# Longer DMA rows, three output places and a later logits load in a top-2 expert dispatch kernel

## The chip, the cores and the metric

The kernel runs on one core of a Trainium2 chip. The metric is device time in microseconds, the median of several runs. Before the change it is 243.29 us (three runs, 243.09 to 243.54). The core has engines that compute (here VectorE, called DVE, and a little ScalarE, called ACT), an engine that issues transfers (SyncE, called SP), and 16 DMA engines that move data between HBM and the on-chip memory (SBUF, 128 partitions). TensorE is not used.

## The reference

`x` is 16 x 1024 tokens of 512 floats, `router_logits` has 8 floats for each token, and `k` is 2. For each token the two largest of the 8 softmax values are taken, normalised to sum to one, and the token's row of `x` is written out twice, once times each of the two weights:

```python
probs = np.exp(router_logits - logits_max)
probs = probs / np.sum(probs, axis=-1, keepdims=True)
topk_indices = np.argsort(probs, axis=-1)[..., -k:]
topk_probs = np.take_along_axis(probs, topk_indices, axis=-1)
topk_probs = topk_probs / np.sum(topk_probs, axis=-1, keepdims=True)
x_expanded = x[:, :, np.newaxis, :].repeat(k, axis=2)
return (x_expanded * topk_probs[..., np.newaxis]).astype(np.float32)
```

So 33.55 MB of `x` and 0.52 MB of logits are read and 67.11 MB are written. With two values left, the normalised weights are the sigmoid of plus and minus their difference, and that is how the kernel gets them.

## The kernel before

The 16,384 tokens are laid over the 128 partitions, 128 consecutive tokens to each, so a partition reads one contiguous stretch of 256 KB of `x` and writes one contiguous stretch of 512 KB of the output. A "row" below is one token's 512 floats (2 KB) in every partition.

The logits are loaded first (L76, 512 KB, 4 KB for each partition). `top2_weights` finds the two largest logits of each token by a tree of max and min on DVE (L26 to L39), and two sigmoids on ACT (L41, L42) write the weights `WA` for all rows at once.

Then two groups of 64 rows follow. In each, eight loads (L84) bring 8 rows each, a 2 MB transfer with 16 KB for each partition, into eight tiles `xg`. After them sixteen products (L90) make 4 rows of output each: `xg`, repeated twice, times `WA`, into one of four tiles `og` (128 x 4096 floats, 2 MB). After each product a store (L98) writes its 2 MB, again 16 KB for each partition. Reads and writes of HBM thus alternate in long phases: 64 rows in, 128 rows out, 64 in, 128 out.

All transfers are issued by SP in the order of the program. A transfer waits at SP until what it needs is done, and those behind it wait too. Once issued, it is split over the 16 DMA engines, 8 partitions to each, and every engine works through its share in the order of issue. The waits are worked out by the tile framework from which parts of which tiles the instructions read and write: a store waits for its product, a product for its load and for the store that last used its `og`, a load of the second group for the products that read the `xg` it overwrites. The framework also gives the transfers eight completion counters in turn, so that a transfer waits for the one eight places before it.

Of the kernel before, what the change touches and what calls it, by code (L numbers as in the profile page):

```python
# [1 line left out]

# [4 lines left out]

F32 = mybir.dt.float32
ALU = mybir.AluOpType
ACTF = mybir.ActivationFunctionType  # L10
P = 128


def top2_weights(nc, pool, logits, M, E):

    hi, lo, n = None, None, E
    while n > 1:  # L20
        n //= 2
        if hi is None:
            a, b = logits[:, :, 0:n], logits[:, :, n : 2 * n]
            nhi = pool.tile([P, M, n], F32, tag=f"hi{n}")
            nlo = pool.tile([P, M, n], F32, tag=f"lo{n}")
            nc.vector.tensor_tensor(nhi, a, b, op=ALU.max)  # L26
            nc.vector.tensor_tensor(nlo, a, b, op=ALU.min)  # L27
        else:
            a, b = hi[:, :, 0:n], hi[:, :, n : 2 * n]
            nhi = pool.tile([P, M, n], F32, tag=f"hi{n}")  # L30
            nlo = pool.tile([P, M, n], F32, tag=f"lo{n}")
            tmp = pool.tile([P, M, n], F32, tag=f"tmp{n}")
            nc.vector.tensor_tensor(tmp, lo[:, :, 0:n], lo[:, :, n : 2 * n], op=ALU.max)  # L33
            nc.vector.tensor_tensor(nlo, a, b, op=ALU.min)  # L34
            nc.vector.tensor_tensor(nlo, nlo, tmp, op=ALU.max)  # L35
            nc.vector.tensor_tensor(nhi, a, b, op=ALU.max)  # L36
        hi, lo = nhi, nlo
    dlt = pool.tile([P, M], F32, tag="dlt")
    nc.vector.tensor_tensor(dlt, hi[:, :, 0], lo[:, :, 0], op=ALU.subtract)  # L39
    WA = pool.tile([P, M, 2], F32, tag="WA")  # L40
    nc.scalar.activation(WA[:, :, 0], dlt, ACTF.Sigmoid, scale=-1.0)  # L41
    nc.scalar.activation(WA[:, :, 1], dlt, ACTF.Sigmoid, scale=1.0)  # L42
    return WA


@with_exitstack
def kernel(
    ctx: ExitStack,
    tc: tile.TileContext,
    x: bass.AP,  # L50
    router_logits: bass.AP,
    k: bass.AP,
    out: bass.AP,
):
    nc = tc.nc
    B, S, D = x.shape
    E = router_logits.shape[-1]
    N = B * S
    assert int(k) == 2 and E == 8 and N % P == 0
    M = N // P  # L60

    L = 8
    H = 4
    GROUP = 8
    x_v = x.rearrange("b s d -> (b s) d").rearrange("(p m) d -> p m d", p=P)
    o_v = out.rearrange("b s k d -> (b s) k d").rearrange("(p m) k d -> p m k d", p=P)
    rl_v = router_logits.rearrange("b s e -> (b s) e").rearrange(
        "(p m) e -> p m e", p=P
    )

    wpool = ctx.enter_context(tc.tile_pool(name="wpool", bufs=1))
    xbufs = ctx.enter_context(tc.tile_pool(name="xbufs", bufs=GROUP))
    obufs = ctx.enter_context(tc.tile_pool(name="obufs", bufs=4))

    logits = wpool.tile([P, M, E], F32)
    nc.sync.dma_start(logits, rl_v)  # L76
    WA = top2_weights(nc, wpool, logits, M, E)

    for g in range(M // L // GROUP):
        chunks = range(g * GROUP, (g + 1) * GROUP)  # L80
        xgs = []
        for c in chunks:
            xg = xbufs.tile([P, L, D], F32, tag="xg")
            nc.sync.dma_start(xg, x_v[:, c * L : (c + 1) * L, :])  # L84
            xgs.append(xg)
        for c, xg in zip(chunks, xgs):
            for h in range(L // H):
                rows = slice(c * L + h * H, c * L + (h + 1) * H)
                og = obufs.tile([P, H, 2, D], F32, tag="og")
                nc.vector.tensor_tensor(  # L90
                    og,
                    xg[:, h * H : (h + 1) * H, :]
                    .unsqueeze(2)
                    .to_broadcast([P, H, 2, D]),
                    WA[:, rows, :].unsqueeze(3).to_broadcast([P, H, 2, D]),
                    op=ALU.mult,
                )
                nc.sync.dma_start(o_v[:, rows], og)  # L98


# [1 line left out]
_INS = ['x', 'router_logits', 'k']  # L102
_OUTS = [((16, 1024, 2, 512), 'float32')]

_NUMBERS = {'k': 2}


# [26 lines left out]
```

## Time and profile before

| | us |
|---|---|
| median of the runs | 243.29 |
| the profiled execution, its own time | 243.44 |
| its span | 241.7 |
| time outside the span (243.44 less 241.7) | 1.7 |
| DVE busy | 144.8 |
| of it, 32 products | 141.1 |
| ACT busy | 1.8 |
| packets of the transfers' queue, as time on 16 engines | 98.9% of the span |

The page that the profile gives lists the busy time of the engines, cuts the span into 40 slices of 6.04 us with the busy share of the DMA engines and the rate at which they move data, and follows the chain of work that ended last. A timeline lists instructions in order of time. Below the page the trace has a record for each DMA packet (its start, duration and size) and for each landing, that is, each completion that a DMA engine reports. A packet here is one partition's contiguous piece of one transfer. A transfer has landed when all 16 engines have reported.

### The profile page before, as it was taken

Reading aid. Unit: us, or ns where it says so; the run is one execution under the profiler, and the core shown is the slowest. Engines: PE = TensorE matmul, PEld = TensorE weight load, DVE = VectorE, ACT = ScalarE, POOL = GpSimd, SP = SyncE. Lnnn points to the kernel's source line nnn. Section 1 sums busy time; section 2 is a strip of 40 time slices with the busy share of each in tenths; the row PEclk is TensorE's granted clock in tenths of the full one; section 3 lists DMA queues with packets and bytes.
Section 4 is the critical chain, followed back from the end, with each engine's and each line's share of the span. In section 5 each row is a group of like instructions: output and inputs, shape, how many; then the busy total and the mean of one; then the engine's idle time right before and its main releaser. Section 6 shows DMA issues by size and latency. Waiting matters only on the chain.

```text
span 241.7 us, 202 instructions
## 1 busy us (share of the span) xinstructions
DVE 144.8 (60%) x43; ACT 1.8 (1%) x3; POOL 0.2 (0%) x4
## 2 busy tenths in 40 slices
DVE  2899400078999899980007991001998989989300
ACT  2000000000000000000000000000000000000000
POOL 0000000000000000000000000000000000000000
DMA  7999999999999999999999999999999999999995
GB/s 274 420 431 434 434 434 369 404 428 434 428 434 434 428 426 431 431 434 431 434 401 428 431 434 426 423 420 431 434 434 434 431 431 427 431 434 433 431 428 233
DMA packets 7058, 101.21 MB, mean 419 GB/s; under 512 B 784, under 2 KB 784, under 8 KB 912
## 3 DMA queue, kind: packets, MB, share of 16 engines
q1 hardware_dynamic: 7056, 101.19, 98.9%
q14 instruction: 2, 0.02, 0.0%
HBM read 34.08 MB, written 67.11 MB: 419 GB/s over the span
## 4 chain that ended last, share of the span: by engine, by line
DMA 74%; DVE 17%; issue 2%; SPq 1%; DVEq 0%
DMA out_dram<-og 61%; DVE og L90 17%; DMA xg<-in_x_dram 13%; SPq L84 0%; SPq L76 0%; SPq L98 0%; DVEq L90 0%
## 5 line engine op out<-in xcount | busy, mean ns | idle before, releaser
L90 DVE TENSOR_TENSOR og<-xg,WA 128x4096 f32<-128x4096 f32 x32 | 141.1, 4423 | 76.5 <-issue 45.5
L26 DVE TENSOR_TENSOR nhi<-logits 128x512 f32<-128x512 f32 x1 | 0.7, 691 | 4.6 <-DMA logits<-in_router_logits_dram 4.6
L41 ACT ACT_TABLE_LOAD x1 | 1.3, 1283 | 0.7 <-PEq L115 0.7
L36 DVE TENSOR_TENSOR nhi<-nhi 128x256 f32<-128x256 f32 (+1 forms) x2 | 0.7, 350 | 0.0
L34 DVE TENSOR_TENSOR nlo<-nhi 128x256 f32<-128x256 f32 (+1 forms) x2 | 0.7, 350 | 0.0
L33 DVE TENSOR_TENSOR tmp<-nlo 128x256 f32<-128x256 f32 (+1 forms) x2 | 0.7, 350 | 0.0
L35 DVE TENSOR_TENSOR nlo<-nlo,tmp 128x256 f32<-128x256 f32 (+1 forms) x2 | 0.7, 350 | 0.0
L27 DVE TENSOR_TENSOR nlo<-logits 128x512 f32<-128x512 f32 x1 | 0.7, 684 | 0.0
L41 ACT ACTIVATE WA<-dlt 128x128 f32<-128x128 f32 x1 | 0.3, 315 | 6.4 <-DVE dlt L39 6.4
L39 DVE TENSOR_TENSOR dlt<-nhi,nlo 128x128 f32<-128x128 f32 x1 | 0.3, 292 | 0.0
L42 ACT ACTIVATE WA<-dlt 128x128 f32<-128x128 f32 x1 | 0.3, 298 | 0.0
L115 POOL MEMSET const-uint8-127<- 128x1 uint8 x1 | 0.1, 103 | 0.0
L115 POOL MEMSET const-bfloat16-1.0<- 128x1 bf16 x1 | 0.1, 102 | 0.0
L115 POOL MEMSET const-float32-0.0<- 128x1 f32 x1 | 0.1, 99 | 0.2 <-issue 0.2
L115 POOL MEMSET const-float32-1.0<- 128x1 f32 x1 | 0.1, 99 | 0.0
## 6 DMA issues: line engine op xcount, KB each, us to landing
out_dram<-og SPq DMA_DIRECT2D x32, 2048.0 KB, 14.9
xg<-in_x_dram SPq DMA_DIRECT2D x16, 2048.0 KB, 28.8
logits<-in_router_logits_dram SPq DMA_DIRECT2D x1, 512.0 KB, 3.8
```

The lines of the kernel that those rows point to most:

```text
L26: nc.vector.tensor_tensor(nhi, a, b, op=ALU.max)
L27: nc.vector.tensor_tensor(nlo, a, b, op=ALU.min)
L33: nc.vector.tensor_tensor(tmp, lo[:, :, 0:n], lo[:, :, n : 2 * n], op=ALU.max)
L34: nc.vector.tensor_tensor(nlo, a, b, op=ALU.min)
L35: nc.vector.tensor_tensor(nlo, nlo, tmp, op=ALU.max)
L36: nc.vector.tensor_tensor(nhi, a, b, op=ALU.max)
L39: nc.vector.tensor_tensor(dlt, hi[:, :, 0], lo[:, :, 0], op=ALU.subtract)
L41: nc.scalar.activation(WA[:, :, 0], dlt, ACTF.Sigmoid, scale=-1.0)
L42: nc.scalar.activation(WA[:, :, 1], dlt, ACTF.Sigmoid, scale=1.0)
L90: nc.vector.tensor_tensor(og, xg[:, h * H : (h + 1) * H, :] .unsqueeze(2) .to_broadcast([P, H, 2, D]), WA[:, rows, :].unsqueeze(3).to_broa ...
L115: nc = _bacc.Bacc("TRN2", target_bir_lowering=False, num_devices=1)
```

## The change

The loads become four of 32 rows, with 64 KB for each partition (8 MB each), and the stores sixteen of 8 rows, with 32 KB for each partition (4 MB each). The products double in size as well (128 x 8192 floats) and halve in number, to 16. The phases stay as they are: 64 rows in, their outputs out, twice.

The 64 rows of a group now lie in one tile `xs` (128 KB for each partition). Outputs rotate over three places: two in a tile `osp` (2 x 32 KB) and a third that is rows 0 to 15 of `xs` itself, which the products 0 and 1 of the group have read by the time that product 2 writes there. The load of rows 0 to 31 of the second group therefore has to wait for the store that last read the third place, product 5's.

The logits are loaded second, behind the first 8 MB of `x` and ahead of the second; `top2_weights` itself is unchanged.

```diff
-    L = 8
-    H = 4
-    GROUP = 8
+    GROUP = 64
+    LX = 32
+    LO = 8
...
-    xbufs = ctx.enter_context(tc.tile_pool(name="xbufs", bufs=GROUP))
-    obufs = ctx.enter_context(tc.tile_pool(name="obufs", bufs=4))
+    logits = wpool.tile([P, M, E], F32)
+    xs = wpool.tile([P, GROUP, D], F32)
+    osp = wpool.tile([P, 2 * LO, 2, D], F32)
 
-    logits = wpool.tile([P, M, E], F32)
-    nc.sync.dma_start(logits, rl_v)
-    WA = top2_weights(nc, wpool, logits, M, E)
+    places = [
+        osp[:, :LO],
+        osp[:, LO:],
+        xs[:, : 2 * LO, :].rearrange("p (r k) d -> p r k d", k=2),
+    ]
 
-    for g in range(M // L // GROUP):
-        chunks = range(g * GROUP, (g + 1) * GROUP)
-        xgs = []
-        for c in chunks:
-            xg = xbufs.tile([P, L, D], F32, tag="xg")
-            nc.sync.dma_start(xg, x_v[:, c * L : (c + 1) * L, :])
-            xgs.append(xg)
-        for c, xg in zip(chunks, xgs):
-            for h in range(L // H):
-                rows = slice(c * L + h * H, c * L + (h + 1) * H)
-                og = obufs.tile([P, H, 2, D], F32, tag="og")
-                nc.vector.tensor_tensor(
-                    og,
-                    xg[:, h * H : (h + 1) * H, :]
-                    .unsqueeze(2)
-                    .to_broadcast([P, H, 2, D]),
-                    WA[:, rows, :].unsqueeze(3).to_broadcast([P, H, 2, D]),
-                    op=ALU.mult,
-                )
-                nc.sync.dma_start(o_v[:, rows], og)
+    WA = None
+    for g in range(M // GROUP):
+        m0 = g * GROUP
+        for h in range(0, GROUP, LX):
+            nc.sync.dma_start(xs[:, h : h + LX, :], x_v[:, m0 + h : m0 + h + LX, :])
+            if WA is None:
+                nc.sync.dma_start(logits, rl_v)
+                WA = top2_weights(nc, wpool, logits, M, E)
+        for n, r in enumerate(range(0, GROUP, LO)):
+            rows = slice(m0 + r, m0 + r + LO)
+            og = places[n % 3]
+            nc.vector.tensor_tensor(
+                og,
+                xs[:, r : r + LO, :].unsqueeze(2).to_broadcast([P, LO, 2, D]),
+                WA[:, rows, :].unsqueeze(3).to_broadcast([P, LO, 2, D]),
+                op=ALU.mult,
+            )
+            nc.sync.dma_start(o_v[:, rows], og)
```

## The prediction

> **What bounds the kernel now.** I read the page first: busy shares, slices, queues. The transfers' queue keeps the 16 DMA engines occupied for 98.9% of the span; DVE, at 60%, is the only other engine with real work.
>
> ```profile
> DVE 144.8 (60%) x43; ACT 1.8 (1%) x3; POOL 0.2 (0%) x4
> DMA  7999999999999999999999999999999999999995
> GB/s 274 420 431 434 434 434 369 404 428 434 428 434 434 428 426 431 431 434 431 434 401 428 431 434 426 423 420 431 434 434 434 431 431 427 431 434 433 431 428 233
> DMA packets 7058, 101.21 MB, mean 419 GB/s; under 512 B 784, under 2 KB 784, under 8 KB 912
> q1 hardware_dynamic: 7056, 101.19, 98.9%
> ```
>
> The slices show a flat 428 to 434 GB/s through reads and writes alike, and a few weak ones. Against 434, a slice of 6.04 us that moved R GB/s lost 6.04 x (434 - R)/434. The first slice lost 2.2 us (start), the seventh and eighth 0.9 and 0.4 (around 40 us), the twenty-first 0.5 (around 121 us, writes turning to reads), the last 2.8 (end). The rest lost a little each. So at most some 7 us lie outside steady moving, and most of that is start and end.
>
> The timeline then says why DVE does not matter: each product waits for a store to free its tile (start, duration, then the idle time before it and what ended it), and a store period is 59.83 - 54.97 = 4.86 us against 4.42 of product.
>
> ```profile
> 9.49 17.43 DVE L90 TENSOR_TENSOR og<-xg,WA 128x4096 f32<-128x4096 f32 x4 [1.14 <-DMA xg<-in_x_dram]
> ...
> 54.97 4.42 DVE L90 TENSOR_TENSOR og<-xg,WA 128x4096 f32<-128x4096 f32 x1 [0.44 <-DMA out_dram<-og]
> 59.83 4.42 DVE L90 TENSOR_TENSOR og<-xg,WA 128x4096 f32<-128x4096 f32 x1 [0.43 <-DMA out_dram<-og]
> 64.69 4.43 DVE L90 TENSOR_TENSOR og<-xg,WA 128x4096 f32<-128x4096 f32 x1 [0.44 <-DMA out_dram<-og]
> ```
>
> Last, the trace's packet records. In steady stretches a 16 KB packet starts 607 ns after the one before it on its engine, in stores and mostly in loads; the 4 KB logits packets start 155.5 ns apart. Two points make a line: (607 - 155.5)/12288 = 36.74 ns per KB (1000 bytes), that is 27.2 GB/s for an engine and 435 for 16, plus **5.0 ns for each packet whatever its size**. A completion costs some 6 ns more. The sum 384 x 607 ns + 8 x 155.5 + 49 x 6 is 234.6 us per engine. The first packet starts at 1.75, the last ends at 240.46, so 4.1 us are loss: the slow start, packets stretched to 0.7 to 1.4 us at 40 to 43 us (1.2 us an engine) and at 121 us (0.4), small ones, and a last engine about 1.2 us behind the rest.
>
> **The change, part by part.** Bytes and phases are the same, and all moves through the same engines, so an edit counts only by what it does to DMA packets or by DMA time left empty.
>
> Loads: 16 x 8 = 128 packets per engine become 4 x 8 = 32 of 64 KB. 96 fewer x 5.0 ns = -0.48 us. Stores: 256 become 128 of 32 KB. 128 x 5.0 = -0.64 us. Completions: 49 transfers become 21, 28 x 6 ns = -0.17 us. Together **-1.3 us**. The line is fitted between 4 and 16 KB; no row shows 32 or 64 KB, nor that such a row stays one packet. Bounds: 0.2 us saved if rows are cut into 16 KB packets again, 1.3 if not. I take 1.3, because every row of the trace up to 16 KB is one packet (7056 = 48 x 128 + 128 + 49 x 16).
>
> Here two rules of the Trainium skill are worth weighing, both on the page "DMA: Bandwidth & Descriptors". Its section "Anatomy of one DMA" gives about 2.0 us fixed per transfer plus bytes at 436 GB/s; 28 fewer transfers would be 56 us less if that were paid serially. The trace contradicts this for a filled queue: transfers of 2 MB follow each other at 4.86 us, which is 8 x 607 ns and 6 ns. Its section "Why small descriptors are slow" has about 3 cycles per packet; at the page's 850 MHz that is 3.5 ns, an estimate that would make the 224 packets worth 0.8 us in place of the 1.1 from the rows.
>
> Logits second: the same packets in another order. The first packets of the run take 0.56 to 0.76 us instead of 0.16, and the windows of the first 6 us move 27, 365 and 403 GB/s. The latency at the head stays with whatever comes first; what may go is the mixing of small packets with the first loads. Bounds 0 and -0.5 us (the two windows' loss, 2 x (69 + 31)/434); I take **-0.1**, nearer zero since the late first byte is most of it.
>
> What logits second delays: `WA`. Logits plus the first four loads, the same bytes in another order, landed at 24.1 us. From logits landed to weights ready took 8.90 - 4.56 = 4.3 us (eleven DVE instructions and two sigmoids), so the weights are there at 28.4 instead of 8.9. The first product, at most 2 x 4.42 = 8.85 us (the trees' rows, 691 ns for 512 and 417 for 256 elements, put some 0.15 us of fixed part in each, so 8.7), ends at 37.2. Its store goes out 0.33 us of issue and about 1 us to its first packet later (0.73 to 1.75 for the first transfer of all), at 38.6. The loads ahead of it keep the engines busy to 43.8, and the second product ends at 46 while the first store runs to 53. Cost **0**, covered by the second 8 MB load with 5 us to spare; beyond those, every us late is a us of empty DMA.
>
> Three places: a 4 MB store takes 2 x 4.86 = 9.7 us. When store n lands, product n+3 may start, and its store is needed when n+1 and n+2 have gone, 19.4 us later; it is there after 8.85 + 1.4 = 10.3. Cost 0, 9 us to spare. With two places alone the same sum would be 10.3 against 9.7, a hole of 0.6 us per store; the third place is that cover.
>
> New wait at SP: the second group's first load needs store 5 landed, since it overwrites the third place. Behind it at SP stand the other load and the group's stores; no other engine issues transfers. Product 7 has by then run (its place came free one store earlier), so stores 6 and 7, 19.4 us, are in the engines' queues when the load is issued. Cost 0, some 18 us to spare. Before, DMA engines had the four last stores queued, as many us.
>
> Second group: its first product waits for an 8 MB load instead of a 2 MB one (four landings of 4.9, so 14.7 us later), and is still covered: 8.85 + 1.4 against the 19.4 us of the second load. DVE's own total falls by 16 x 0.15 us, off the path.
>
> The other stalls: at 40 us all engines' packets stretch together within the last load, before the first store's packets, with DVE idle. I can't tie it to anything the change touches, so it stays, between -1.2 (gone) and, if a stretched packet is stretched in proportion to its length, +1.2 (doubled for stores) to +3.6 (fourfold for loads). Likewise 0.4 at 121 us: -0.4 to +1.3. I take 0 for both, since the records tie neither to packet size. End: the last landing, drain and the lagging engine are as before; packets twice as long could leave the engines up to one 32 KB packet more apart, 0 to +0.6, taken as 0.
>
> Sum: -1.3 - 0.1 = -1.4 us on the profiled 243.44 (span 241.7 and 1.7 around it): 242.0. The median of the runs is 0.15 below that execution, so 241.9; I say **242.0**, leaving 0.1 for the end.
>
> **The rivals.**
>
> *Rows are cut again.* If a 64 or 32 KB row goes out as 16 KB packets, only completions and the start are left: -0.2 to -0.3 us, 243.0. For it: no row over 16 KB is in the trace. Against: nothing up to 16 KB was cut.
>
> *The turns get dearer (the other side).* One engine's queue holds packets in order; where reads meet writes, packets stretched from 0.61 to 0.7-0.85 us at 121 us, and to 1.1-1.4 at 40 us. If a stall lasts as long as the packets caught in it, it grows with their length: +1.7 us if the 1.2 and 0.4 merely double, +4.9 if loads' fourfold length counts throughout. With -1.4 that is 243.6 to 246.8. It decides from stalls 1.4 us longer in sum, somewhat under a doubling. For it: in both places two or three whole packets on each engine are long. Against: at 160 us, reads to writes again, the records show almost nothing (0.1 us), and in time, not in packets, nothing says that a stall must grow.
>
> *The stall at 40 us goes with the order of the loads.* Then 1.2 more is saved: 240.7. For it: it is one event in 240 us and the other turn of its kind lacks it. Against: nothing in the profile names its cause.
>
> *Long transfers wait on a late first store.* It needs the weights over 5 us later than worked out, and none of the rows gives that; I count it into the dearer turns' share.
>
> **How the numbers follow.** Forecast as worked out 0.52; stall gone 0.10; rows cut 0.13; dearer turns or an empty stretch 0.25. The median can tell about 0.2%, 0.5 us: faster means under 242.8, slower over 243.8. The forecast's own range is 241.4 to 242.6 and, like the stall gone, wholly faster; rows cut is within; of the dearer turns some 0.22 lies above 243.8 and 0.03 within. Faster 0.62, same 0.16, slower 0.22. For 8 in 10 the range leaves out half of the stall gone, below 240.9, and the dear half of the turns, above 244.6.
>
> **What would show it.** Right: packets of 64 KB at about 2413 ns and 32 KB at 1209 ns an engine; a store period of 9.68 us, not 9.73; slices of 432 to 435; DMA packets about 3,000 in place of 7,058 (32 x 16 + 128 x 16 + 128 + 21 x 16 = 3,024); no slice below 425 besides start, end, 40 and 121 us; the first product at about 28 us and the first store issued well before 43. Wrong: a gap in the DMA row after 42 or 160 us (late products), stretches longer than 1.2 and 0.4 us where reads and writes meet, or 7,000 packets again. The forecast would fail most simply if the per-packet cost didn't fall with the count, since that is nearly all of the gain.

## The result

The changed kernel takes 243.17 us (median of four runs, 242.75 to 243.45), the kernel before beside it 243.19. The ratio is 0.9997 with an interval of 0.9976 to 1.0019: no change that this comparison can tell. A second comparison, with five and 23 runs, gave 242.99 against 242.19, ratio 1.0033 (1.0021 to 1.0045): there the changed kernel is a third of a per cent slower. The forecast of 242.0, faster, did not come true. Below, every ratio is against runs of the kernel before on the same chip, and on the chips of the experiments that kernel took 242.2 to 242.4 us.

The page of the changed kernel, same lines as those shown of before:

```profile
DVE 142.5 (59%) x27; ACT 1.8 (1%) x3; POOL 0.2 (0%) x4
DMA  8999899899999999999999898989999999999995
GB/s 348 392 479 435 359 511 348 354 430 435 435 435 435 435 435 435 435 435 435 430 354 522 348 522 348 522 310 435 435 430 435 430 435 435 430 424 435 435 435 239
DMA packets 3024, 101.19 MB, mean 420 GB/s; under 512 B 336, under 2 KB 336, under 8 KB 464
q1 hardware_dynamic: 3024, 101.19, 98.5%
```

The packets fell from 7,056 to the 3,024 that the prediction had counted, so no row is cut. In the write phases (slices 9 to 19 and 28 to 39) the rate is 435 in most slices, 424 at the least, where it was 426 to 434. In the read phases it swings between 310 and 522. That is bookkeeping: a 64 KB packet lasts 2.4 us, and 522 is more than any steady stretch moves, so bytes are put down to a slice that did not carry all of them. With long packets these slices can no longer show a weak spot, and the packet records have to. So the prediction's sign "no slice below 425" can't be read here.

From the timeline of the changed kernel (start, duration, instruction; SPq is the issue of a transfer):

```profile
23.99 0.69 DVE L26 TENSOR_TENSOR nhi<-logits 128x512 f32<-128x512 f32 x1 [23.99 <-DMA logits<-in_router_logits_dram]
28.34 17.29 DVE L93 TENSOR_TENSOR osp<-xs,WA 128x8192 f32<-128x8192 f32 x2 [0.58 <-ACT WA L42]
37.06 8.94 SPq L99 DMA_DIRECT2D out_dram<-osp  x2
...
63.94 8.69 DVE L93 TENSOR_TENSOR osp<-xs,WA 128x8192 f32<-128x8192 f32 x1 [0.97 <-DMA out_dram<-osp]
73.63 8.69 DVE L93 TENSOR_TENSOR xs<-xs,WA 128x8192 f32<-128x8192 f32 x1 [1.00 <-DMA out_dram<-xs]
...
102.59 1.35 SPq L86 DMA_DIRECT2D xs<-in_x_dram  x2
142.41 17.30 DVE L93 TENSOR_TENSOR osp<-xs,WA 128x8192 f32<-128x8192 f32 x2 [40.74 <-DMA xs<-in_x_dram]
```

All the covers hold: logits at 24.0, first product at 28.3, first store issued at 37.1 while loads run to 44. Store periods are 73.63 - 63.94 = 9.69 us, and the second group's loads go out at 102.6 with two stores still queued. In the packet records the engines are never without work between 34 and 48, 100 and 130 or 150 and 168 us. So in these stretches nothing is lost to waits, and the loss must lie inside the packets.

**Where the time is.** An account of one profiled execution can be made from the packet and landing records. *Nominal* is the sum of packets at their steady period and 6 ns for each completion. *Stretch* is what packets lasted beyond the usual duration of their size, summed and divided by 16. *Spread* is the last engine's report of the last store less the mean of the 16 reports. *Rest* is what is left up to that mean (landing delay, small gaps). The kernel before and the changed one were profiled twice each; the last column, the changed kernel with the logits first and a last store of the first group in short packets, is an experiment told below.

| us | before | before, again | changed | changed, again | short last store |
|---|---|---|---|---|---|
| first packet | 1.75 | 1.73 | 1.74 | 1.74 | 1.75 |
| nominal | 234.66 | 234.66 | 233.44 | 233.44 | 233.57 |
| stretch | 2.54 | 1.79 | 3.31 | 3.37 | 2.15 |
| of it 0 to 6 us | 0.57 | 0.38 | 0.49 | 0.66 | 0.30 |
| 34 to 48 (reads to writes) | 1.22 | 1.02 | 1.13 | 1.31 | 1.29 |
| 114 to 130 (writes to reads) | 0.46 | 0.12 | 1.09 | 0.58 | 0.06 |
| 150 to 168 (reads to writes) | 0.16 | 0.09 | 0.58 | 0.80 | 0.47 |
| rest | 0.63 | 0.86 | 0.71 | 0.52 | 0.79 |
| spread | 1.23 | 0.62 | 0.77 | 1.34 | 0.51 |
| after the last report | 2.63 | 2.64 | 2.78 | 2.78 | 2.59 |
| time | 243.44 | 242.30 | 242.75 | 243.19 | 241.36 |

Averaged over the two traces each, the nominal sum fell by 1.22 us, as predicted, and the stretch rose by 3.34 - 2.17 = 1.17. The two later turns gave back 0.55 and 0.57 of it. The remaining terms add 0.15 us, and the times differ by 242.97 - 242.87 = 0.10. Single traces differ by 0.75 in stretch and 0.6 in spread for the same kernel, which is why one pair of profiles (here 0.7 us faster) says little.

The records also show which packets are stretched. Where loads and stores differ in packet size, they can be told apart. At 40 and at 158 us, where reads turn to writes, all of the stretch then lies in load packets, the last ones before the stores: in the changed kernel one 64 KB packet on each engine. At the turn from writes to reads it is shared: of the 1.09 us in the changed kernel's first trace, 0.61 lies in 19 store packets and 0.48 in 30 load packets behind them.

### The profile page after: what moved, and what is told of

Read it like the earlier page. It is cut to its first block, busy times and chain, and to the rows that moved or that the text cites. A ratio compares the mean times of both kernels' runs of the same rounds, so it can differ in the third digit from the quotient of the medians.

```text
span 241.0 us, 119 instructions
## 1 busy us (share of the span) xinstructions
DVE 142.5 (59%) x27; ACT 1.8 (1%) x3; POOL 0.2 (0%) x4
## 2 busy tenths in 40 slices
DMA packets 3024, 101.19 MB, mean 420 GB/s; under 512 B 336, under 2 KB 336, under 8 KB 464
## 3 DMA queue, kind: packets, MB, share of 16 engines
q1 hardware_dynamic: 3024, 101.19, 98.5%
## 4 chain that ended last, share of the span: by engine, by line
DMA 60%; DVE 27%; issue 4%; SPq 0%; ACT 0%; ACTq 0%; DVEq 0%
DVE osp L93 18%; DMA out_dram<-osp 18%; DMA xs<-in_x_dram 16%; DMA out_dram<-xs 16%; DMA logits<-in_router_logits_dram 9%; DVE xs L93 7%; DVE nhi L26 0%; DVE nlo L27 0%; DVE nlo L35 0%; DVE tmp L33 0%; DVE nlo L34 0%; DVE nhi L36 0%; SPq L86 0%; ACT WA L41 0%; DVE dlt L39 0%
## 5 line engine op out<-in xcount | busy, mean ns | idle before, releaser
L93 DVE TENSOR_TENSOR osp<-xs,WA 128x8192 f32<-128x8192 f32 x12 | 104.1, 8690 | 51.1 <-DMA xs<-in_x_dram 40.7
L93 DVE TENSOR_TENSOR xs<-xs,WA 128x8192 f32<-128x8192 f32 x4 | 34.8, 8692 | 2.1 <-DMA out_dram<-xs 2.0
```

What stands on the lines that cost most here:

```text
L93: nc.vector.tensor_tensor(og, xs[:, r : r + LO, :].unsqueeze(2).to_broadcast([P, LO, 2, D]), WA[:, rows, :].unsqueeze(3).to_broadcast([P, ...
```

## The experiments

The theory after the result: a packet costs what was worked out, but at a turn between reads and writes the packets in flight are stretched, and more so when they are long.

**The changed kernel again.**

> The changed kernel unaltered, for a second trace and a sharper comparison. Theory (turns): the 1.2 us of per-packet cost is really saved (384 x 607.1 ns + 49 completions before, 32 x 2414.6 + 128 x 1209.4 ns + 21 completions now), and 0.8 us of it is given back by packets stretched where reads and writes meet (3.3 us of stretch per engine now against 2.55 before). Then the stretch is again 3.0 to 3.6 us, in the same three places (about 40, 119 to 124 and 158 us), and the time 0.2 to 0.8 us below before, ratio 0.997 to 0.999. Rival (chance): stretches come and go between executions; then this trace has a total that differs from 3.3 by over 0.6 us, in either direction, and the places differ.

242.99 us, ratio 1.0033 (1.0021 to 1.0045), stretch 3.37 in the same places. The rival falls, for the changed kernel: its stretch is not a chance of one execution. The time was forecast wrong; it is slower than before there, since the kernel before has less stretch and spread in its second trace, told next, than in its first.

**The kernel before again.**

> The kernel before, unaltered, for its trace on the chip of the last runs, where it took 242.19 us and the changed kernel 242.99 in place of 243.2 for both. Theory (turns): the packets are as on the other chip (607.1 ns each, 234.7 us an engine), so it is 0.8 us faster than the changed kernel there only if its stretch is some 2 us an engine less than the changed kernel's 3.4, or its engines end closer together; stretch 1.4 to 2.0 us. Rival: stretch of 2.5 us as in the first trace, and the difference lies in the spread of the engines' ends (1.9 us between first and last report of the last store in both kernels so far).

242.35 us. Stretch 1.79, as the theory had it, and spread 0.62, against 3.37 and 1.34 in the changed kernel's second trace: 1.6 and 0.7 us, less 1.2 of nominal sum, is 1.1, where the two times are 0.9 apart. Both terms make the difference, not one. (This run was on another chip than the changed kernel's, and each is one execution.)

**Logits first, the rest as changed.**

```diff
-            if WA is None:
-                nc.sync.dma_start(logits, rl_v)
-                WA = top2_weights(nc, wpool, logits, M, E)
...
+    nc.sync.dma_start(logits, rl_v)
+    WA = top2_weights(nc, wpool, logits, M, E)
```

> The changed kernel with one part undone: logits loaded first, then the two 8 MB loads. Theory (turns): the order of the logits is worth nothing beyond the head of the run, 0 to 0.3 us slower than the changed kernel. Rival (order): the late logits and late products cost something that hid the gain; then this is faster than the changed kernel by 0.5 us or more, with the stretches at 40 us or 158 us gone.

242.61 us, ratio 1.0016 (1.0008 to 1.0025), so 0.4 us faster than the changed kernel on that chip, with intervals that overlap by a little. I had expected it the same or slower. The stretches at 40 and 158 us are not gone (1.39 and 0.75), so the rival's way is not it either. What the trace shows is a start with 0.21 us of stretch instead of 0.66 and a spread of 0.70 instead of 1.34, in one execution each.

**Loads back to 16 KB packets; stores back to 16 KB packets.** The two edits, in that order:

```diff
-    LX = 32
+    LX = 8
...
-            if WA is None:
+            if WA is None and h == 24:
```

> The changed kernel with only the loads back to 8 rows (16 KB packets, 128 per engine; logits still behind the first 32 rows), stores at 32 KB. Per-packet cost: 96 x 5 ns + 12 completions x 6 ns = +0.55 us. Theory (turns): the stretch inside loads goes back to what 16 KB packets showed (123 us: 0.4 to 0.15; 158 us: 0.6 to 0.1; 40 us unchanged at 1.1), -0.6 to -0.7, so in sum 0 to 0.2 us below the changed kernel. Rival (stretch does not follow packet length): the full +0.55 us.

```diff
-            nc.sync.dma_start(o_v[:, rows], og)
+            for q in range(0, LO, 4):
+                nc.sync.dma_start(
+                    o_v[:, m0 + r + q : m0 + r + q + 4], og[:, q : q + 4]
+                )
```

> The changed kernel with each 4 MB store issued as two of 4 rows (16 KB packets, 256 per engine), loads at 64 KB. Per-packet cost: 128 x 5 ns + 16 completions x 6 ns = +0.74 us. Theory (turns): the stretch of the last stores at 119 us falls from 0.55 to about 0.3, the rest stays, so 0.5 us above the changed kernel. Rival (stretch does not follow packet length): +0.74 us.

With short loads 242.42 us, ratio 1.0009 (1.0001 to 1.0018): 0.6 us faster than the changed kernel, although its packets cost 0.5 more. Sign as the theory, size beyond it. The stretch is 2.49; at 40 us it fell too, to 0.62. With short stores 243.23 us, ratio 1.0046 (1.0034 to 1.0058): 0.2 us slower than the changed kernel where 0.5 and 0.74 had been named; the stretch at 114 to 130 us is 0.27, as forecast. By these two runs long loads cost more than they save, and long stores about pay for themselves.

**Long stores alone** (logits first, loads of 8 rows, stores of 8 rows; the edit is `LX = 8` in the kernel with logits first).

> One part of the change alone: stores of 32 KB packets with products of 8 rows in three places; loads of 8 rows (16 KB packets) and logits first, as before. Per-packet cost against before: 128 x 5 ns + 16 completions x 6 ns = -0.74 us. Theory (turns): only the one turn from writes to reads sees longer packets, +0.1 to +0.3 us, so 0.4 to 0.6 us faster than before. Rival (32 KB stores give their gain back as well): 0 to 0.2 us slower than before, as the changed kernel with 16 KB loads is (242.42 against 242.19).

242.23 against 242.28, ratio 0.9994 (0.9984 to 1.0004): between the two expectations, and no change. The kernel before was profiled on the same chip, so the account is direct: nominal 0.71 less (233.95), stretch 0.62 more (2.41 against 1.79), of it 0.48 at the turn from writes to reads and 0.21 at 158 us, although no 64 KB packet is left in this kernel.

**More turns.** Eight groups of 16 rows, loads one group ahead, in packets of 16 or 32 KB:

```diff
-    GROUP = 64
-    LX = 32
-    LO = 8
+    GROUP = 16
+    LX = 8    # 16 in the second kernel
+    LO = 4    # 8 in the second kernel
...
+    load(0)
+    nc.sync.dma_start(logits, rl_v)
+    WA = top2_weights(nc, wpool, logits, M, E)
+    for g in range(M // GROUP):
+        if g + 1 < M // GROUP:
+            load(g + 1)
...
+            nc.sync.dma_start(o_v[:, rows], og)
```

> Eight groups of 16 rows in place of two of 64, loads one group ahead of the stores: 13 turns between reads and writes in place of 3. Packets of 16 KB both ways, as before (128 + 256 per engine, 49 completions: 234.7 us). It computes the same output. Theory (turns): each turn stretches packets by some 0.58 us an engine (1.75 over 3 turns in the trace of before), so 10 more turns add 5.8 us: 248. Rival (stretches are no matter of turns but of moments, as 40 us): no more than 1 us above before.

> The same 13 turns with packets of 32 KB both ways (64 + 128 per engine, 25 completions: 233.6 us). It computes the same output. Theory (turns, longer with longer packets: 0.9 us a turn in the changed kernel with 64 and 32 KB against 0.58 with 16): 0.7 to 0.8 us a turn, so 1 us of stretch per 13 turns more for each 0.08, in sum 0.5 to 2 us slower than the same kernel with 16 KB packets. Rival (a turn costs the same whatever the packet): 1.1 us faster than it.

246.73 and 250.77 us. Ten more turns with 16 KB packets cost 4.4 us, of which 0.7 is a gap at the first store (time with no packet between 20 and 34 us): 0.4 us a turn, less than the 0.58 forecast, and far above the rival's 1 us in all. Against the trace of before on the same chip the 4.4 us are 2.3 of stretch, 1.6 of spread and 0.5 of rest, so a good part is engines that end apart and not longer packets. The second number was misread at first sight: its page has a hole. The slices and, from the timeline, the first issue of stores:

```profile
DMA  8895599999999989999999999999999999999994
GB/s 315 385 477 252 252 420 421 368 431 352 447 457 426 420 352 442 442 442 389 442 431 436 431 363 442 447 452 420 421 420 436 436 420 399 431 436 436 436 426 179
```

```profile
27.20 8.95 SPq L102 DMA_DIRECT2D out_dram<-osp  x2
```

The second load had landed at 23.8 and the first store went out at 27.2: empty queues in slices 4 and 5, which my own experiment had caused by putting the logits second behind a short load. So it was run again with the logits first:

```diff
-    load(0)
     nc.sync.dma_start(logits, rl_v)
+    load(0)
```

> The 13-turn kernel with 32 KB packets both ways once more, with the logits first: with logits second its first store came 4.8 us after the second load had ended (a hole at 24 to 29 us), which was no matter of turns. That hole gone, 246.0. Against the 13-turn kernel with 16 KB packets (246.7, of it 0.4 of such a hole), theory: per-packet cost -1.06 is given back by stretch longer by 1.3 us (4.8 against 3.5 beyond the start, in the traces), so 246.0 to 246.6. Rival (a turn costs the same whatever the packet): 245.2 to 245.5.

247.13 us, above both expectations. Its nominal sum is 1.06 below the kernel with 16 KB packets, and it is 0.4 slower. Its stretch is hardly longer (4.26 against 4.09; without the first 6 us 0.5 longer, where 1.3 was expected); its spread is 0.9 longer (3.16 against 2.22) and its rest 0.4. So in these two kernels, with two runs and one trace each, packets of 32 KB lose what they save and more, but mainly as engines that end apart and short gaps; the growth of a turn's stretch is at most a part of it.

**The long loads last or first.** Same packets, other order:

```diff
-        for h in range(0, GROUP, LX):
-            nc.sync.dma_start(xs[:, h : h + LX, :], x_v[:, m0 + h : m0 + h + LX, :])
+        cuts = (0, 8, 16, 24, 32, 64)    # second kernel: (0, 32, 40, 48, 56, 64)
+        for h, e in zip(cuts, cuts[1:]):
+            nc.sync.dma_start(xs[:, h:e, :], x_v[:, m0 + h : m0 + e, :])
```

> Logits first, stores of 32 KB packets, and in each group the loads are 8, 8, 8, 8 and then 32 rows: the 64 KB packets stand right before the stores. Against the next kernel the packets are the same in number and size, only their order differs (233.6 us an engine for both, 1.05 below before). Theory (a turn stretches the packets in flight, the outgoing direction's last ones, the more the longer they are): stretch at 40 us some 1.3 and at 158 us 0.7, as with 64 KB loads so far, and 0.4 to 1.0 us slower than the next kernel: 242.3 to 242.8 where before takes 242.3. Rival (the long loads cost wherever they stand, or not at all): within 0.2 us of the next kernel.

> The same packets in the other order: in each group 32 rows first, then 8, 8, 8, 8, so 16 KB packets stand before the stores. Theory: stretch at 40 us some 0.9 and at 158 us 0.25, as with 16 KB loads so far; 0.3 to 0.6 us faster than before, as the 32 KB stores still stand before the turn to reads. Rival: within 0.2 us of the kernel with the long loads last.

242.69 (ratio 1.0017, 1.0008 to 1.0026) and 242.38 (1.0001, 0.9992 to 1.0010). Long loads last are 0.3 us slower, between the two expectations (0.4 at the least, 0.2 at the most); the second kernel, expected 0.3 to 0.6 us faster than before, is no faster. The stretch does not bear the theory's reason out: at 40 us 1.27 and 1.03, but at 158 us 0.66 and 0.81, although 16 KB packets stand there in the second kernel. So for turns from reads to writes the length of the last loads alone does not decide, as far as one trace each can tell.

**Short packets ahead of every turn.** Logits first, and:

```diff
+        cuts = (0, 32, 48, 56, 60, 64) if g == 0 else (0, 8, 32, 48, 56, 60, 64)
...
+            if g == 0 and r + LO == GROUP:
+                for q in range(0, LO, 2):
+                    nc.sync.dma_start(
+                        o_v[:, m0 + r + q : m0 + r + q + 2], og[:, q : q + 2]
+                    )
+            else:
+                nc.sync.dma_start(o_v[:, rows], og)
```

> Long packets away from the turns, short ones ahead of them: logits first; loads of 32, 16, 8, 4, 4 rows in the first group and 8, 24, 16, 8, 4, 4 in the second; stores of 32 KB packets, but the last store of the first group is issued as four of 2 rows (8 KB packets). 240 packets and 31 completions an engine: 233.8 us, 0.9 below before. Theory: stretch no more than in before (1.8 here), rather 1.2 to 1.6 with 8 KB packets at the turns, so 0.8 to 1.5 us faster than before, 240.8 to 241.5. Rival (stretch does not depend on the packets at the turn, 2.4 to 3.3 whatever is done): 0 to 0.6 us slower than that, 241.9 to 242.9.

241.40 us, ratio 0.9966 (0.9953 to 0.9978): faster than the kernel before and, by ratio, than the changed one. Stretch 1.75, no more than in before, so the packets' saving is kept; at 114 to 130 us it is 0.00 and at 158 us 0.08. At 40 us it is still 1.16.

**Its two halves.** The last store alone cut into four (the lower part of the diff, loads of 32 rows), and the loads alone (the upper part):

> Logits first, loads of 32 rows throughout (64 KB packets), stores of 32 KB; only the last store of the first group is issued as four of 2 rows (8 KB packets). 24 packets and 3 completions more than the changed kernel: +0.14 us. Theory (the stretch at a turn goes with the length of the outgoing packets): the stretch from 114 to 130 us, 0.6 to 1.1 so far with 32 KB stores before the turn, falls to 0 to 0.2; the one at 158 us stays at 0.7. So 0.5 to 0.8 us faster than the changed kernel with logits first (242.6): 241.8 to 242.1. Rival (it is the incoming 64 KB loads): stretch at 114 to 130 us unchanged, 242.6 to 242.8.

> The other half of the tapered kernel: loads of 32, 16, 8, 4, 4 rows in the first group and 8, 24, 16, 8, 4, 4 in the second, all stores of 32 KB. Theory (outgoing): stretch from 114 to 130 us stays at 0.6 or so, since 32 KB stores stand before that turn; the one at 158 us is near 0.1, since 8 KB loads stand before that one. So 0.4 to 0.7 us slower than the tapered kernel (241.4): 241.8 to 242.1. Rival (incoming): the stretch at 114 to 130 us is gone too, as the loads behind the turn are short, and the time is that of the tapered kernel within 0.2 us.

The store alone: 241.44 us, ratio 0.9967 (0.9955 to 0.9979), better than forecast and as good as both halves together. The loads alone: 242.69 us, ratio 1.0014 (1.0005 to 1.0023), no gain at all, where 241.8 to 242.1 had been expected; the stretch at 114 to 130 us stayed at 0.77, so short packets behind the turn do not help and the rival falls. At 158 us it was 0.44, where 0.1 had been expected. The whole gain over the kernel with logits first comes from 4 MB out of 101 that leave in short packets. On the page of the kernel with the short last store:

```profile
DMA packets 3456, 101.19 MB, mean 422 GB/s; under 512 B 384, under 2 KB 384, under 8 KB 512
q1 hardware_dynamic: 3456, 101.19, 98.7%
```

432 records more than the changed kernel (384 packets and 48 completions), 0.13 us an engine. Against the kernel with logits first, profiled on another chip, stretch fell by 1.12 (3.27 to 2.15, of it 0.86 at this turn and 0.28 at 158 us) and spread by 0.19; the ratios 1.0016 and 0.9967 are 1.2 us apart. At this turn the load packets are no longer stretched either (0.01 us), though they still are 64 KB long.

Two things change with the packets here: the store is four transfers in place of one, and the loads behind it are issued later. The issue of both, in the kernel with the short last store, and of the loads in the kernel before:

```profile
101.69 3.53 SPq L99 DMA_DIRECT2D out_dram<-osp  x4
105.32 2.11 SPq L87 DMA_DIRECT2D xs<-in_x_dram  x2
```

```profile
108.43 15.28 SPq L84 DMA_DIRECT2D xg<-in_x_dram  x8
```

The changed kernel issued its loads at 102.59. The issue time alone does not order the stretch: the kernel before issues its loads latest of all, and has 0.46 and 0.12 there against 0.06. The number of transfers is not told apart from the length of the packets: in every kernel here shorter packets came as more transfers.

**The long load away from the turn behind which it stood** (second group's cuts 0, 8, 40, 48, 56, 64 in the kernel with the long loads first).

> The kernel with the long loads first, except that the second group's loads are 8, 32, 8, 8, 8 rows in place of 32, 8, 8, 8, 8: the same packets, and the 64 KB ones no longer stand right behind the turn from writes to reads. Theory (outgoing packets alone set the stretch): no difference from that kernel (242.38) beyond 0.2 us, stretch at 158 us as there, 0.8. Rival (long packets behind a turn put the engines out of step and that is paid at the next turn): stretch at 158 us falls to 0.3 or less, 0.4 to 0.6 us faster, 241.8 to 242.0.

242.59 us, ratio 1.0014 (1.0006 to 1.0023), stretch at 158 us 0.76. Unchanged there, so the rival falls; the time lies 0.3 us above the other kernel's by ratio, on another chip, without a reason that I can show.

**The opposite of the cure: a longer last store.**

```diff
+            if g == 0 and r + 2 * LO == GROUP:
+                continue
+            if g == 0 and r + LO == GROUP:
+                nc.sync.dma_start(o_v[:, m0 + r - LO : m0 + r + LO], osp)
+            else:
+                nc.sync.dma_start(o_v[:, rows], og)
```

> Logits first, loads of 64 KB packets, stores of 32 KB packets, except that the last two stores of the first group are issued as one of 16 rows (64 KB packets) after product 7, which is the opposite of cutting the last store into 8 KB packets (241.44). That store is issued at most 0.5 us after the engines have finished the one before it, so up to 0.5 us can be lost there by empty queues, seen as a gap and not as stretch. Theory (stretch goes with the length of the last store's packets): stretch from 114 to 130 us 1.4 to 2.0 us, in place of 0.9 with 32 KB, and 0.5 to 1.0 us slower than the same kernel with 32 KB there (242.61), beside the gap: 243.1 to 244.1. Rival (anything from 16 KB up costs alike): stretch 0.6 to 1.1, 242.5 to 243.1.

The store, in the timeline:

```profile
101.72 0.33 SPq L100 DMA_DIRECT2D out_dram<-osp  x1
```

244.03 us, ratio 1.0072 (1.0058 to 1.0086), 1.4 us above the kernel with 32 KB there. The two traces are 1.15 apart: 0.7 us an engine is the gap before that store (time with no packet between 100 and 116 us), and 0.37 is stretch at this turn. That stretch is 1.29, a little under the 1.4 named and above the 0.57 to 1.09 of nine traces with 32 KB. So the direction holds from 8 to 64 KB, at its upper end by one trace in which the engines had run empty before the store, and doubling the length does not double the stretch.

**The packet cost without turns.** Both kernels read the logits and 8 rows of `x`, make two products and store one place to all rows; loads, products and most of the arithmetic are left out.

```diff
+    LS = 4    # 16 in the second kernel
+    nc.sync.dma_start(xs[:, :LO, :], x_v[:, :LO, :])
...
+    for r in range(0, M, LS):
+        nc.sync.dma_start(o_v[:, r : r + LS], osp[:, :LS])
```

> Leaves out most of the computation: the logits, the weights and 8 rows of x are read, two products are made, and then all 128 rows of output are stored from that one place, 32 stores of 4 rows (16 KB packets, 256 per engine), so only the time of the stores is to be read. One turn at the start. The stores alone are 256 x 607.1 ns + 32 completions = 155.6 us an engine. It is the measure for the next kernel.

> The same with 8 stores of 16 rows (64 KB packets, 64 per engine): 64 x 2414.6 ns + 8 completions = 154.6 us an engine. Theory (5.0 ns for each packet is device time): 1.0 to 1.2 us faster than the same with 16 KB packets. Rival (the per-packet cost is hidden by something else that ends last): within 0.3 us of it.

The times, 179.42 and 185.77 us, look like a loss of 6.3. The issue of the stores explains it; first the kernel with 16 KB packets, then the one with 64:

```profile
18.07 119.74 SPq L94 DMA_DIRECT2D out_dram<-osp  x32
```

```profile
26.67 8.29 SPq L94 DMA_DIRECT2D out_dram<-osp  x8
```

A store of 16 rows needs both products, one of 4 rows only the first, which I had not set even. The first store packet starts at 18.91 and 27.52, the last ends at 176.34 and 182.70: 157.43 against 155.18 us. The stream is 2.2 us shorter with 192 packets and 24 completions fewer per engine, twice the 1.0 to 1.2 forecast, and it reaches the device time: 27.52 - 18.91 = 8.61 later, 6.35 slower. So the rival falls: without a turn behind it, the packets' cost is time. The excess has a part that the records show: the packets of these streams last longer than in the other kernels, 615 against 611 ns with 16 KB and 2,422 against 2,418 with 64, and 4 ns on each of 256 and of 64 packets are 1.0 and 0.3 us. Why they do stays open, and so this pair does not measure the 5 ns for a packet by itself.

## Why the prediction was wrong, point by point

- *Packets and completions, -1.3 us: right.* 32 and 64 KB packets start 1209.4 and 2414.6 ns apart (1209 and 2413 foretold) and 16 KB ones 607.1, so a packet done away with saves 4.8 ns up to 32 KB and 4.6 up to 64 KB; 1.22 us of nominal sum. The stores-only kernels show a saving of this sign as time, though twice as large.
- *The two rules of the Trainium skill ("DMA: Bandwidth & Descriptors").* The estimate of 3.5 ns from the 3 cycles of "Why small descriptors are slow" is too low here: the rows decide. The 2.0 us of "Anatomy of one DMA" are a fit for transfers issued from GpSimd, as that section says. This kernel issues from SP, so its 4.86 us a transfer neither contradict nor confirm that fit.
- *The slices, "at most some 7 us" outside steady moving: too low.* The formula given there, summed over all forty slices, makes 8.5. Nothing in the forecast rests on it.
- *Logits second, -0.1: wrong in sign, as far as it can be told.* Undoing it won 0.4 us with long loads. With 16 KB loads the ratio is 1.0009 with logits second and 0.9994 with logits first, on two chips. The covers of `WA` and of the first store held (28.4 foretold, 28.3 measured), so the cost is not a late product; what it is stays open.
- *Three places, the new wait at SP, the second group's cover, all 0: right.* No engine ran dry between 10 and 236 us (0.002 us an engine without a packet in the one trace, none in the other).
- *The other stalls, taken as 0 because "the records tie neither to packet size": the step that failed.* The stall at 120 us grew by 0.55 and that at 158 us by 0.57, together most of the saving. One of the signs named for being wrong, a stretch longer than 0.4 us at the turn from writes to reads, is in both traces (1.09 and 0.58). The rival of the dearer turns, which had 0.25, was the one that came, at +1.2 us of stretch and a little more spread. Its stated size, +1.7 for a doubling, was too much at 40 us, where the stall did not grow, and it had nothing for 158 us: I held the quiet turn there against it, and that turn is half of what was given back.
- *The stall at 40 us, taken as unchanged: right in the main.* It is 1.22 and 1.02 us in before and 1.13 and 1.31 in the changed kernel. Over all kernels with these phases it is 0.6 to 1.2 us where 16 KB loads stand there, 1.05 and 1.16 with 8 KB, 1.1 to 1.5 with 64 KB, so it is far from growing with the packets' length: 8 KB packets go from 309 to some 600 ns one after the other, one 64 KB packet from 2,418 to some 3,700. What causes it no run shows.
- *Rows cut again: did not happen.* *The end, 0 to +0.6, taken as 0: small.* The spread is 0.13 us longer on average, less than two traces of one kernel differ, and the time after the last report 0.15.

What is shown: what the turn from writes to reads costs goes with the packets of the last store, and with the logits loaded first, shortening those alone turns the change from 0.16% slower into a gain of 0.33%. Whether it is their length or the number of transfers is not shown. What is not settled: why the second turn from reads to writes has more stretch in kernels with 64 KB loads (0.47 to 0.81) than in before (0.09 and 0.16), since 16 KB packets right ahead of it did not help (0.81, 0.76) and 8 KB ones did in one kernel (0.08) and half in another (0.44). It is not the 64 KB loads alone: with loads of 16 KB throughout and stores of 32 KB it is 0.45 and 0.30. And the cost of the logits' order, 0.4 us in two pairs of kernels, stays open.

## What to carry to other kernels

When a kernel keeps its DMA engines full, longer rows save a few nanoseconds for each packet they do away with, and that sum can be made closely from two packet sizes in the trace (1.3 us foretold, 1.2 counted). But look at the turns between reading and writing as well: what stands last before a turn from writes to reads should be short. For turns from reads to writes these runs give no such rule. Judge half a per cent by many runs beside each other and by an account of the packets, not by one pair of profiles.

## What the runs showed of the hardware

- The stretch of packets at the turn from writes to reads, by the last store's packets: 0.00 and 0.06 us an engine with 8 KB, 0.12 to 0.46 with 16 KB, 0.57 to 1.09 with 32 KB, 1.29 with 64 KB (one trace). With 32 KB part of it lies in the loads behind the turn; at turns from reads to writes all of it lies in the last loads.
- Engines stay together without turns and drift apart with them: from first to last report of the last store 0.3 and 0.2 us in the stores-only kernels, 1.0 to 2.0 with three turns, 3.5 to 4.7 in three traces with 13 (from the landing records).
- Packets start 155.3, 607.1, 1209.4 and 2414.6 ns apart on an engine with 4, 16, 32 and 64 KB in the kernels that read and write, each row up to 64 KB being one packet, and a completion takes 6 ns.
- A rate by slices swings by half when packets last a good part of a slice (348 and 522 GB/s in neighbours), so a low slice is a stall only if its neighbour is not as much too high.
